# Handing the second halves of a split and part of a weight scaling to GpSimd, with copies a tick later, in a one-core attention layer

## The chip, the cores and the metric

The kernel runs on one core of a Trainium2 chip. The core has a matrix engine (TensorE: PE for its matmuls, PEld for its weight loads), VectorE (DVE), ScalarE (ACT) and GpSimd (POOL). Each works through its own list of instructions in order, and an instruction starts when the semaphores that it names have been set. SyncE (SP) only issues DMA transfers, in order as well; POOL and ACT issue some too. The metric is the time of one execution in device microseconds.

## The reference

One decoder layer on 2048 tokens of width 1024. The input is RMS-normalised and modulated, then projected at once to the inputs of two attention mixers. Mixer A ("FoX") is causal softmax attention of 8 heads of width 64 with a bias from cumulated forget gates. Mixer B is sliding-window attention (128 keys) with 8 query heads, 2 key heads, rotary positions and a sink per head. Both outputs are gated, joined and sent through `w_out`; the result is RMS-normalised, gated and added to the input.

```python
proj = h @ w_in[l]
qa, ka, va, fa, za, qb, kb, vb, zb = jnp.split(proj, split_points, axis=-1)
oa = forgetting_attention(...)          # causal, 8 heads
oa = oa * jax.nn.silu(za)
ob = sliding_window_sink_attention(...) # window 128
ob = ob * jax.nn.silu(zb)
y = jnp.concatenate([oa, ob], axis=-1) @ w_out[l]
x = x + gate[:, None, :] * rms_norm(y, g_post[l])
```

## The kernel before

Every f32 matrix is held as two f16 planes: an upper part (the value rounded to f16) and a lower part (what the rounding left). A product of two such matrices is three f16 matmuls. An upper part is one ACT instruction, a lower part one DVE instruction that subtracts the upper part from the value. The change deals with who makes these parts, and when.

The program is written out by hand, and each engine keeps the order in which the code issues instructions. Work that follows a product is put off with `after(n, f)`: `tick()` counts all such entries down by one and runs those that are due, in the order of their registration.

Three stages matter here.

The *banded stage* is mixer B. Its loop runs over 32 windows (`Pair`: one pair of heads, two blocks of 128 queries). A window has four ticks, with pieces of the projections (`fill`) between them: after the first tick `maxima` (DVE scans L884 and the small L887), after the second `pv` of the window two before (PE L933 into the single PSUM tile `pob`), after the third `exps` (ACT L895) and `split`, which puts off the upper part of the probabilities `sp` (ACT L912) by one tick and the lower part (DVE L917) by two. The window's result goes from `pob` to `on` (DVE L939), is copied to the upper part of `oh` (ACT L948), gets its lower part (DVE L949), and `put` (POOL L945) stores both to `o_d` in DRAM. The projections' weights pass `w_load`, `w_max`, `w_back`, `w_scale`, `w_high` (ACT L273), `w_low` in two halves (DVE L279) and `w_done`; `leads` in `add` says how many pieces (`punits`) ahead of their first use each is issued. POOL also multiplies the rotated halves by the sines (L735), copies the sinks (L882) and issues several DMAs.

The *FoX stage* is mixer A, 8 heads of 20 steps. A step (`Step`) has the scores of two key blocks (PE L1343 and L1344 into the single tile `sta`), the exponential (ACT L1348), for blocks on the diagonal a mask (POOL L1352), the upper part `pha` (ACT L1356), the lower part (DVE L1359), and two steps later `pv` (PE L1369 to L1372 into the single tile `poa`). At the last step of each quarter of the queries (`ci`, of 2, 4, 6 and 8 steps) the result goes to `ona` (DVE L1378), `oha` (ACT L1385, DVE L1386), and by SP (L1382) to `o_d`. A step has two ticks: one behind the exponential, one behind the scores of the next step.

*Head 7*, the last 20 steps, also readies the output product. `w_out` is loaded in 16 pieces (`w_out_load`, SP L1454) and split by `w_out_split`: upper part on ACT (L1459), lower part on DVE (L1460); the table `w_at` says at which step `r` each is split, and the load comes three steps earlier. The first output blocks of 128 rows are readied: `load_o` fetches the planes of `o_d` by transposing DMAs (SP L1475), and `turn` joins them (DVE L1493), multiplies by the gate (DVE L1497), sums squares (ACT L1500), and makes upper and lower parts `oz` (ACT L1511, DVE L1514) for the products (PE L1530).

Last comes the output stage, of which the change touches nothing.

Of the kernel before, what the change touches and what calls it, by code (L numbers as in the profile page):

```python
# [18 lines left out]
P = 128  # L19
# [21 lines left out]
def hybrid_layer(  # L41
# [146 lines left out]
    def after(n, f):  # L188
        late.append([n, f])
# [662 lines left out]
    class Pair:  # L852
# [73 lines left out]
        def pv(self):  # L926
# [10 lines left out]
            def out_():  # L937
                on = onp.tile([P, 2, P], F32, tag="on", name="on")
                V.tensor_tensor(on[:].rearrange("p e (h d) -> p (e h) d", h=2), po[:],  # L939
                                self.rinv[:].unsqueeze(2).broadcast_to([P, 4, 64]), op=ALU.mult)  # L940
                oh = onp.tile([P, 2, 2, P], F16, tag="oh", name="oh")

                def put():
                    rows_ = slice(2 * (i % 4) * P, 2 * (i % 4 + 2) * P)
                    G.dma_start(o_d[i // 4][rows_, (4 + j) * P:(5 + j) * P].rearrange("(m p) c -> p m c", p=P),  # L945
                                oh[:].rearrange("p e a c -> p (e a) c"))

                after(1, lambda: A.activation(oh[:, :, 0], on[:], AF.Copy))  # L948
                after(3, lambda: V.tensor_tensor(oh[:, :, 1], on[:], oh[:, :, 0], op=ALU.subtract))  # L949
                after(4, put)  # L950

            after(1, out_)
# [5 lines left out]
    def add(key, us):  # L958
        if key not in pkeys and key not in ("kb", "vb"):
# [3 lines left out]
                  lambda: w_high(key), lambda: w_low(key, 0), lambda: w_low(key, 1), lambda: w_done(key))  # L963
            if key[:2] == "za":
                leads = leads[:1] + tuple(n - 5 for n in leads[1:])
            if at > N_PRO and (key == "qk0" or key[:2] not in ("qk", "za")):
                leads = (58 if key == "qk0" else 64,) + leads[1:]
            for n, f in enumerate(fs):
# [356 lines left out]
    class Step:  # L1325
# [35 lines left out]
        def pv(self):  # L1361
# [12 lines left out]
            if self.last:  # L1374
                rinv = sm(4, "a_ri")
                V.reciprocal(rinv[:], po[:, :, 64])
                on = op_.tile([P, 4, 64], F32, tag="ona", name="ona")
                V.tensor_tensor(on[:], po[:, :, 0:64], rinv[:].unsqueeze(2).broadcast_to([P, 4, 64]), op=ALU.mult)  # L1378
                oh = op_.tile([P, 4, 2, 64], F16, tag="oha", name="oha")

                def put():
                    SP.dma_start(o_d[self.ci][:, hd * 64:(hd + 1) * 64].rearrange("(m p) d -> p m d", p=P),  # L1382
                                 oh[:].rearrange("p u a d -> p (u a) d"))

                after(1, lambda: A.activation(oh[:, :, 0], on[:], AF.Copy))  # L1385
                after(2, lambda: V.tensor_tensor(oh[:, :, 1], on[:], oh[:, :, 0], op=ALU.subtract))  # L1386
                after(3, put)

        po_ = {}

# [20 lines left out]
    def w_slot(n):  # L1411
        return oio["w"][:, n // KT, n % KT, :]
# [42 lines left out]

    def w_out_split(m):
        k, cc = m % KT, slice((m // KT) * CH, (m // KT + 1) * CH)
        raw, hi = w_raw.pop(m), w_slot(k)[:, cc]
        A.activation(hi, raw, AF.Copy, scale=wsc[:, k:k + 1])  # L1459
        V.scalar_tensor_tensor(w_slot(8 + k)[:, cc], raw, wsc[:, k:k + 1], hi, op0=ALU.mult, op1=ALU.subtract)  # L1460

    class Out:

# [162 lines left out]
    with tc.manual_schedule():  # L1626
# [18 lines left out]
        for _ in range(3):  # L1645
# [2 lines left out]
        p0, p_tot = pos[0], len(punits) - pos[0] - P_LEAD - P_LAST  # L1648
        m_ramp, m_from, m_done = 0, 6 * NS + 7, 7 * NS + 3

        w_at = {2: [0], 3: [1], 4: [2], 5: [3], 6: [4], 8: [5], 10: [6], 11: [7], 12: [8], 13: [9], 14: [10],
                15: [11, 12], 16: [13, 14], 17: [15]}
        w_all = sum(s.w for s in steps[:7 * NS])
        w_acc = 0
        lag[0] = 4
        for s, stp_ in enumerate(steps):
# [43 lines left out]
            tick()  # L1700
            if s >= PV_LAG:
                steps[s - PV_LAG].pv()
            for u in todo[half:]:
                u()
            if r == 3 and hd + 1 < 8:
# [5 lines left out]
                    w_out_load(m)  # L1711
            if hd == 7 and r in (1, 2):
                outs[r - 1].load_z()
            if hd == 7 and r in (5, 6):
                outs[r - 5].load_o()
            if hd == 7 and r in (7, 9):
                outs[(r - 7) // 2].turn(4)
            if s % 4 == 1 and s // 4 <= 32:
# [54 lines left out]
```

## Time and profile before

| | us |
|---|---|
| median of 3 runs | 1162.84 (1162.61 to 1162.91) |
| the profiled execution | 1161.38 |
| its span, first to last instruction | 1159.6 |
| banded stage, about | 205 to 412 |
| FoX stage with its preparation, about | 412 to 923 |
| head 7, about | 923 to 1006 |

The page's second part cuts the span into 40 slices of 29 us. A digit is the busy share of an engine in tenths; PEclk is the granted clock of TensorE, DMA the busy share of the 16 DMA engines.

```profile
PE   5899999989999999999999999999999978999997
DVE  6776568888898858889998899978888878888885
ACT  4666445556665543676767767776776669533331
POOL 2011222233332211111111111102100000000000
PEclk9999999989999999999999999999999999999999
DMA  9646426566788932243323332223212158688853
```

PE is at nine tenths nearly throughout. Dips outside the start stand in the ninth slice (where the clock dips as well) and in the 33rd and 34th, which are head 7. DVE is at eight tenths, POOL nearly idle.

### The profile page before, as it was taken

Reading aid. Unit: us, or ns where it says so; the run is one execution under the profiler, and the core shown is the slowest. Engines: PE = TensorE matmul, PEld = TensorE weight load, DVE = VectorE, ACT = ScalarE, POOL = GpSimd, SP = SyncE. Lnnn points to the kernel's source line nnn. Section 1 sums busy time; section 2 is a strip of 40 time slices with the busy share of each in tenths; the row PEclk is TensorE's granted clock in tenths of the full one; section 3 lists DMA queues with packets and bytes.
Section 4 is the critical chain, followed back from the end, with each engine's and each line's share of the span. In section 5 each row is a group of like instructions: output and inputs, shape, how many; then the busy total and the mean of one; then the engine's idle time right before and its main releaser. Section 6 shows DMA issues by size and latency. Waiting matters only on the chain.

```text
span 1159.6 us, 26925 instructions
## 1 busy us (share of the span) xinstructions
PE 1106.1 (95%) x10386; PEld 638.6 (55%) x10386; DVE 949.7 (82%) x2394; ACT 694.1 (60%) x1188; POOL 174.7 (15%) x317
## 2 busy tenths in 40 slices
PE   5899999989999999999999999999999978999997
PEld 1466657545468956555555555555555545544443
DVE  6776568888898858889998899978888878888885
ACT  4666445556665543676767767776776669533331
POOL 2011222233332211111111111102100000000000
PEclk9999999989999999999999999999999999999999
DMA  9646426566788932243323332223212158688853
GB/s 330 220 138 168 108 69 129 103 149 133 141 153 112 130 85 73 63 113 74 82 68 84 88 74 74 59 53 78 64 39 61 29 135 198 153 202 195 197 172 109
DMA packets 210324, 136.35 MB, mean 118 GB/s; under 512 B 145276, under 2 KB 189348, under 8 KB 210196
## 3 DMA queue, kind: packets, MB, share of 16 engines
q1 hardware_dynamic: 198100, 98.53, 37.8%
q0 software_dynamic: 11616, 35.58, 11.1%
q8 instruction: 81, 1.33, 0.5%
q10 hardware_dynamic: 480, 0.53, 0.2%
q14 instruction: 47, 0.39, 0.1%
HBM read 62.58 MB, written 25.18 MB: 76 GB/s over the span
## 4 chain that ended last, share of the span: by engine, by line
PE 54%; DVE 22%; issue 4%; ACT 4%; DMA 1%; POOL 0%; DVEq 0%; ACTq 0%; POOLq 0%
PE bk L335 18%; PE bk L1530 14%; PE sta L1343 4%; PE sta L1344 4%; PE bk L1294 4%; DVE sp L917 3%; PE poa L1371 2%; PE poa L1372 2%; PE poa L1369 2%; ACT sp L912 2%; DVE a_m L1297 2%; PE bk L353 2%; DVE pha L1359 1%; DVE wmx L230 1%; DVE b_nb L887 1%
## 5 line engine op out<-in xcount | busy, mean ns | idle before, releaser
L1348 ACT ACTIVATE p<-sta,lift,scl_qk 128x1024 f32<-128x1024 f32 (+2 forms) x160 | 171.7, 1073 | 78.8 <-PE sta L1344 74.1
L335 PE MATMUL bk<-hT,wh_qk 128*128 128x512 f16 x768 | 197.9, 378 | 0.0
L1530 PE MATMUL bk<-wohl,oz 128*128 128x512 f16 (+2 forms) x792 | 169.4, 372 | 0.8 <-DVE oz L1514 0.8
L1359 DVE TENSOR_TENSOR pha<-p,pha 128x1024 f16<-128x1024 f32 (+2 forms) x160 | 169.9, 1062 | 0.2 <-ACT pha L1356 0.2
L1356 ACT ACTIVATE pha<-p 128x1024 f16<-128x1024 f32 (+2 forms) x160 | 147.7, 923 | 28.5 <-POOL p L1352 25.8
L1297 DVE TENSOR_REDUCE a_m<-bk 128x1 f32<-128x512 f32 x192 | 130.3, 684 | 32.8 <-PE bk L1294 32.3
L1530 PEld LDWEIGHTS <-oz 128*128 128x128 f16 x792 | 76.0, 99 | 85.5 <-DVE oz L1514 1.3
L1369 PE MATMUL poa<-vt,pha 128*128 128x65 f16 x1088 | 117.7, 194 | 3.0 <-DVE ona L1378 3.0
L1343 PE MATMUL sta<-T 128*128 128x512 f16 (+1 forms) x320 | 110.3, 349 | 9.8 <-ACT p L1348 9.8
L1372 PE MATMUL poa<-vt,pha 128*128 128x65 f16 x1088 | 117.2, 193 | 1.3 <-DVE pha L1359 1.3
L1371 PE MATMUL poa<-vt,pha 128*128 128x64 f16 x1088 | 117.5, 195 | 0.0
L1369 PEld LDWEIGHTS <-pha 128*128 128x128 f16 x1088 | 102.5, 97 | 17.5 <-DVE ona L1378 4.0
L1294 PE MATMUL bk<-T 66*128 66x512 f16 (+2 forms) x320 | 110.5, 348 | 0.2
L1371 PEld LDWEIGHTS <-pha 128*128 128x128 f16 x1088 | 101.7, 98 | 13.5 <-issue 0.3
L1344 PE MATMUL sta<-T 69*128 69x512 f16 (+1 forms) x320 | 108.8, 350 | 0.0
L335 PEld LDWEIGHTS <-wh_qk 128*128 128x128 f16 x768 | 70.2, 97 | 70.0 <-issue 1.3
L1372 PEld LDWEIGHTS <-pha 128*128 128x128 f16 x1088 | 101.5, 99 | 1.6 <-DVE pha L1359 1.6
L335 PE MATMUL bk<-hT,wh_za 128*128 128x512 f16 x384 | 101.1, 381 | 0.0
L1352 POOL TENSOR_SCALAR_AFFINE_SELECT p<-p 128x256 f32<-128x256 f32 x64 | 31.6, 494 | 424.8 <-ACT p L1348 412.3
L335 PE MATMUL bk<-hT,wh_qb 128*128 128x512 f16 x384 | 91.1, 385 | 4.4 <-DVE wh_qb L279 4.4
L353 PE MATMUL bk<-wh_va,hT 128*128 128x128 f16 x1536 | 93.1, 219 | 2.0 <-DVE wh_va L279 2.0
L353 PEld LDWEIGHTS <-hT 128*128 128x128 f16 x1536 | 87.6, 98 | 7.3 <-issue 4.9
(501 smaller groups left out, 1905.5 us busy)
## 6 DMA issues: line engine op xcount, KB each, us to landing
hT<-in_x_dram SPq DMA_DIRECT2D x20, 512.0 KB
wa<-in_w_ada_dram SPq DMA_DIRECT2D x16, 512.0 KB
T<-stq SPq DMA_DIRECT2D x128, 64.0 KB
T<-z_d SPq DMA_DIRECT2D x16, 512.0 KB
z_d<-tz POOLq DMA_DIRECT2D x30, 256.0 KB, 3.0
out_dram<-hT POOLq DMA_DIRECT2D x15, 512.0 KB, 5.2
xt<-in_x_dram SPq DMA_DIRECT2D x12, 512.0 KB
qs<-qf SPq DMA_DIRECT2D x80, 64.0 KB
```

The lines of the kernel that those rows point to most:

```text
L335: PE.matmul(ps, whl[:, a, k, :], hT[ci][:, b, k, :], start=(k == 0 and n == 0), stop=(k == KT - 1 and n == 2))
L353: PE.matmul(ps[:, u * P:(u + 1) * P], hT[ci][:, a, k, u * P:(u + 1) * P], whl[:, b, k, :], start=(k == 0 and n == 0), stop=(k == KT - 1 an ...
L1294: PE.matmul(mx[:, :w], T[0:XM, 0, i * P:(i + 1) * P], T[0:XM, 2, pc * CH:pc * CH + w], start=True, stop=True)
L1297: V.tensor_reduce(m3[:, u, pc:pc + 1], mx[:, :w], axis=AX.X, op=ALU.max)
L1343: PE.matmul(self.st[:, o:o + w], T[:, 3, kb_], T[:, 1, qc], start=True, stop=False)
L1344: PE.matmul(self.st[:, o:o + w], T[0:XR, 2, kb_], T[0:XR, 0, qc], start=False, stop=True)
L1348: A.activation(self.p32[:, :self.w], self.st[:, :self.w], AF.Exp, scale=scl[f"qk{self.hd}"][:], bias=lift[:])
L1359: V.tensor_tensor(self.ph[:, 1, :self.w], self.p32[:, :self.w], self.ph[:, 0, :self.w], op=ALU.subtract)
L1369: PE.matmul(po[:, u, :], ph[:, 0, pq], vt[:, b, hd, 0:65], start=(self.first and n == 0 and u == 0), stop=False)
L1371: PE.matmul(po[:, u, 0:64], ph[:, 0, pq], vt[:, b, hd, 65:VW], start=False, stop=False)
L1372: PE.matmul(po[:, u, :], ph[:, 1, pq], vt[:, b, hd, 0:65], start=False, stop=(self.last and n == len(self.blocks) - 1))
L1530: PE.matmul(py, self.hl[:, i, k, :], w_slot(8 * j + k)[:, cc], start=(k == 0 and m_ == 0), stop=(k == KT - 1 and m_ == 2))
```

## The change

Five edits.

1. Banded stage: the lower part of `oh` is made by POOL in `put`, directly ahead of the store that POOL issues. The ACT copy ahead of it comes one tick later.
2. The halves of `w_low` for the projections `qb1` to `qb3` are issued at 8 and 6 pieces ahead of their use, in place of 6 and 4; `w_done` at 5 in place of 3.
3. FoX stage: the lower part of `oha` is made by POOL; copy, lower part and store are each one tick later; and `oha` has two buffers, for even and odd quarters.
4. Head 7: eleven of the sixteen upper parts of `w_out` (all but pieces 0, 2, 3, 6 and 7) are made by POOL. The lower parts stay with DVE, but move from ahead of a step's first pieces to behind its `pv` (`w_out_low`). Pieces 11 and 13 come one step earlier.
5. The planes for the first two output blocks are fetched behind steps 6 and 7, in place of 5 and 6.

```diff
@@ Pair.pv, out_ @@
                 def put():
+                    G.tensor_tensor(oh[:, :, 1], on[:], oh[:, :, 0], op=ALU.subtract)
                     rows_ = slice(2 * (i % 4) * P, 2 * (i % 4 + 2) * P)
                     G.dma_start(o_d[i // 4][rows_, (4 + j) * P:(5 + j) * P].rearrange("(m p) c -> p m c", p=P),
                                 oh[:].rearrange("p e a c -> p (e a) c"))
 
-                after(1, lambda: A.activation(oh[:, :, 0], on[:], AF.Copy))
-                after(3, lambda: V.tensor_tensor(oh[:, :, 1], on[:], oh[:, :, 0], op=ALU.subtract))
+                after(2, lambda: A.activation(oh[:, :, 0], on[:], AF.Copy))
                 after(4, put)
@@ add @@
+            if key[:2] == "qb" and at > N_PRO:
+                leads = leads[:5] + (8, 6, 5)
@@ Step.pv @@
-                oh = op_.tile([P, 4, 2, 64], F16, tag="oha", name="oha")
+                oh = op_.tile([P, 4, 2, 64], F16, tag=f"oha{self.ci % 2}", name="oha")
...
-                after(1, lambda: A.activation(oh[:, :, 0], on[:], AF.Copy))
-                after(2, lambda: V.tensor_tensor(oh[:, :, 1], on[:], oh[:, :, 0], op=ALU.subtract))
-                after(3, put)
+                after(2, lambda: A.activation(oh[:, :, 0], on[:], AF.Copy))
+                after(3, lambda: G.tensor_tensor(oh[:, :, 1], on[:], oh[:, :, 0], op=ALU.subtract))
+                after(4, put)
@@ w_out_split @@
-        raw, hi = w_raw.pop(m), w_slot(k)[:, cc]
-        A.activation(hi, raw, AF.Copy, scale=wsc[:, k:k + 1])
-        V.scalar_tensor_tensor(w_slot(8 + k)[:, cc], raw, wsc[:, k:k + 1], hi, op0=ALU.mult, op1=ALU.subtract)
+        raw, hi = w_raw[m], w_slot(k)[:, cc]
+        if m in (0, 2, 3, 6, 7):
+            A.activation(hi, raw, AF.Copy, scale=wsc[:, k:k + 1])
+        else:
+            G.tensor_scalar(hi, raw, wsc[:, k:k + 1], None, op0=ALU.mult)
+
+    def w_out_low(m):
+        k, cc = m % KT, slice((m // KT) * CH, (m // KT + 1) * CH)
+        V.scalar_tensor_tensor(w_slot(8 + k)[:, cc], w_raw.pop(m), wsc[:, k:k + 1], w_slot(k)[:, cc],
+                               op0=ALU.mult, op1=ALU.subtract)
@@ the loop over steps @@
-        w_at = {2: [0], 3: [1], 4: [2], 5: [3], 6: [4], 8: [5], 10: [6], 11: [7], 12: [8], 13: [9], 14: [10],
-                15: [11, 12], 16: [13, 14], 17: [15]}
+        w_at = {2: [0], 3: [1], 4: [2], 5: [3], 6: [4], 8: [5], 10: [6], 11: [7], 12: [8], 13: [9], 14: [10, 11],
+                15: [12, 13], 16: [14], 17: [15]}
...
             if s >= PV_LAG:
                 steps[s - PV_LAG].pv()
+            if hd == 7:
+                for m in w_at.get(r, []):
+                    w_out_low(m)
...
-            if hd == 7 and r in (5, 6):
-                outs[r - 5].load_o()
+            if hd == 7 and r in (6, 7):
+                outs[r - 6].load_o()
```

The order of PE's own instructions is the same in both programs. Three places elsewhere show what moves.

First place: ACT in the banded stage, at the window whose probabilities `sm__3076` are split. Before, ACT stands so (L895 the exponentials, L273 the upper part of the weights, L912 the upper part of the probabilities):

```order
L895 ACTIVATE sm__3076,b_rs<-sm__3076,b_nb 128x257 x2
L273 ACTIVATE wh_qb_3153<-wr_qb_2330,w_sw 128x1024
L948 ACTIVATE oh<-on 128x2x128
L912 ACTIVATE sp_1978<-sm__3076 128x256
L912 ACTIVATE sp_1978<-sm__3076 128x512
L723 ACTIVATE qf<-bk_139 128x512
```

And now:

```order
L895 ACTIVATE sm__3076,b_rs<-sm__3076,b_nb 128x257 x2
L273 ACTIVATE wh_qb_3153<-wr_qb_2330,w_sw 128x1024
L912 ACTIVATE sp_1978<-sm__3076 128x256
L912 ACTIVATE sp_1978<-sm__3076 128x512
L723 ACTIVATE qf<-bk_139 128x512
L949 ACTIVATE oh<-on 128x2x128
```

The copy `oh<-on` no longer stands between the exponentials and the upper part `sp`; it follows both, ahead of the next window's exponentials.

Second place: DVE, at the same window and the next, whose maxima are scanned by L884 (some rows of equal kind between are left out at the start and the end). Before:

```order
L939 TENSOR_TENSOR on<-pob,b_ri 128x256
L917 TENSOR_TENSOR sp_1979<-sm__3076,sp_1978 128x256
L917 TENSOR_TENSOR sp_1979<-sm__3076,sp_1978 128x512
L921 RECIPROCAL b_ri<-b_rs 128x4
L742 SCALAR_TENSOR_TENSOR qc<-bk_139,cosT 128x512
```

Behind these come the four scans of the next window, and then:

```order
L887 TENSOR_SCALAR b_nb<-b_m 128x2
L279 SCALAR_TENSOR_TENSOR wh_qb_3153<-wr_qb_2330,w_sw,wh_qb_3153 128x512
L736 TENSOR_TENSOR qc<-qc,qs 128x512
L949 TENSOR_TENSOR oh<-on,oh 128x2x128
L279 SCALAR_TENSOR_TENSOR wh_qb_3153<-wr_qb_2330,w_sw,wh_qb_3153 128x512
```

Now the stretch ahead of the scans reads:

```order
L939 TENSOR_TENSOR on<-pob,b_ri 128x256
L279 SCALAR_TENSOR_TENSOR wh_qb_3153<-wr_qb_2330,w_sw,wh_qb_3153 128x512
L917 TENSOR_TENSOR sp_1979<-sm__3076,sp_1978 128x256
L917 TENSOR_TENSOR sp_1979<-sm__3076,sp_1978 128x512
L921 RECIPROCAL b_ri<-b_rs 128x4
```

The first half of `wh_qb` has moved from behind the scans to ahead of L917; the second half stands directly behind the scans, and `oh<-on,oh` has left DVE.

Third place: ACT in head 7, from the upper part of step 2 to the upper part of step 4 (L1348 and L1350 are the exponentials before and now, L1459 and L1462 the parts of `w_out`). Before:

```order
L1459 ACTIVATE wohl<-wo_14210,wsc 128x512
L1356 ACTIVATE pha<-p_14256 128x1024
L1348 ACTIVATE p_14314<-sta,lift,scl_qk_13021 128x1024
L1459 ACTIVATE wohl<-wo_14212,wsc 128x512
L1356 ACTIVATE pha<-p_14314 128x1024
L1348 ACTIVATE p_14349<-sta,lift,scl_qk_13021 128x896
L1385 ACTIVATE oha<-ona 128x4x64
L385 ACTIVATE gz<-bk_139,cz_za_13337 128x512
L1256 ACTIVATE rw<-bk_6465 8x128
L1459 ACTIVATE wohl<-wo_14214,wsc 128x512
L1356 ACTIVATE pha<-p_14349 128x896
```

And now:

```order
L1462 ACTIVATE wohl<-wo_14210,wsc 128x512
L1358 ACTIVATE pha<-p_14256 128x1024
L1387 ACTIVATE oha<-ona 128x4x64
L1350 ACTIVATE p_14313<-sta,lift,scl_qk_13021 128x1024
L1358 ACTIVATE pha<-p_14313 128x1024
L1350 ACTIVATE p_14349<-sta,lift,scl_qk_13021 128x896
L385 ACTIVATE gz<-bk_139,cz_za_13336 128x512
L1258 ACTIVATE rw<-bk_6465 8x128
L1462 ACTIVATE wohl<-wo_14214,wsc 128x512
L1358 ACTIVATE pha<-p_14349 128x896
L1387 ACTIVATE oha<-ona 128x4x64
```

One part of `w_out` has left this stretch of ACT, the copy of head 6's last quarter now stands here (it was just ahead of the stretch), and the copy of head 7's first quarter has moved behind step 4's upper part.

## The prediction

> **What bounds the kernel now.** I cut the span by stage and look at PE's busy time first: the program's PE instructions and their order do not change, so the kernel can only become faster where PE stands idle or runs at a lower clock.
>
> ```profile
> core 0: us, PE busy (x) PEld busy (x) DVE busy (x) ACT busy (x) POOL busy (x), PEclk, DMA share, GB/s
> 231.00:235.00 4.00, 0.20 (x1) 0.00 (x0) 3.93 (x15) 1.62 (x7) 0.30 (x2) 0.78 0.52 100
> 235.00:241.00 6.00, 5.91 (x25) 2.29 (x26) 4.53 (x11) 3.03 (x7) 1.22 (x2) 0.58 0.46 102
> 205.00:412.00 207.00, 195.46 (x2440) 131.17 (x2438) 176.18 (x525) 125.45 (x320) 60.40 (x117) 0.98 0.74 133
> 412.00:923.00 511.00, 506.25 (x4967) 285.05 (x4966) 440.31 (x1009) 345.59 (x478) 65.32 (x115) 1.00 0.29 69
> 923.00:1006.00 83.00, 72.62 (x754) 42.12 (x752) 68.49 (x122) 62.60 (x88) 7.14 (x13) 0.96 0.63 153
> ```
>
> PE idles 207.00 - 195.46 = 11.5 us in the banded stage, 511.00 - 506.25 = 4.8 in the FoX stage and 83.00 - 72.62 = 10.4 in head 7. To this comes the clock: behind the longest stall of the banded stage 6 us were granted 0.58, a loss of 6 x 0.42 = 2.5; head 7 at 0.96 loses about 83 x 0.04 = 3.3. All together 32.5 us, the most that the change could bring. PE's waits say who was late:
>
> ```profile
> PE sta L1343 <- ACT p L1348: 9.8, 9, 2.9
> ...
> PE bk L335 <- DVE wh_qb L279: 4.4, 2, 3.9
> PE poa L1369 <- DVE ona L1378: 3.0, 4, 1.2
> PE pob L933 <- DVE on L939: 2.5, 4, 1.2
> PE bk L353 <- DVE wh_va L279: 2.0, 3, 0.9
> ...
> PE bk L1243 <- DVE vt L362: 1.4, 1, 1.4
> ...
> PE poa L1372 <- DVE pha L1359: 1.3, 2, 1.0
> ...
> PE pob L933 <- DMA ptb<-sp: 1.2, 2, 0.7
> ...
> PE bk L1530 <- DVE oz L1514: 0.8, 1, 0.8
> ```
>
> In the banded stage 4.4 + 2.5 + 2.0 + 1.4 = 10.3 us of the 11.5 fall to DVE and 1.2 to a DMA. DVE is busy for 176.18 of 207 us there, so why is it late? Its own waits and ACT's answer:
>
> ```profile
> DVE sp L917 <- ACT sp L912: 26.7, 22, 1.4
> ...
> ACT oh L948 <- DVE on L939: 23.9, 26, 2.2
> ```
>
> The two form a loop. ACT makes the copy `oh` ahead of `sp` and waits for DVE's `on`; DVE, right behind `on`, then waits for `sp`, up to 1.4 us: the copy (0.42) and `sp` itself (1.04). One window shows it, with the late weights behind:
>
> ```profile
> 228.59 0.42 ACT L948 ACTIVATE oh<-on 128x256 f16<-128x256 f32 x1 [1.00 <-DVE on L939]
> 228.91 0.92 ACT L912 ACTIVATE sp<-sm__3076 128x256 f16<-128x256 f32 x2
> ...
> 229.32 1.26 POOL L735 TENSOR_TENSOR qs<-qs,sinT 128x512 f32<-128x512 f32 x1 [0.70 <-DMA qs<-qf]
> ...
> 229.34 2.12 DVE L917 TENSOR_TENSOR sp<-sm__3076,sp 128x256 f16<-128x256 f32 x2 [0.79 <-ACT sp L912]
> ...
> 234.29 0.74 DVE L279 SCALAR_TENSOR_TENSOR wh_qb<-wr_qb,w_sw,wh_qb 128x512 f16<-128x512 f32 x1
> ```
>
> **Durations.** The operations that leave an engine, and the two POOL operations nearest to the new ones:
>
> ```profile
> L949 DVE TENSOR_TENSOR oh<-on,oh 128x256 f16<-128x256 f32 x32 | 13.4, 418 | 0.0
> L1386 DVE TENSOR_TENSOR oha<-ona,oha 128x256 f16<-128x256 f32 x32 | 13.3, 415 | 0.0
> L1459 ACT ACTIVATE wohl<-hT,wsc 128x512 f16<-128x512 f32 x11 | 7.6, 711 | 0.0
> ...
> L735 POOL TENSOR_TENSOR qs<-qs,sinT x20: 1259/1263/2018, 57.4 to 356.7; 128x512 f32<-128x512 f32 x20
> ...
> L1352 POOL TENSOR_SCALAR_AFFINE_SELECT p<-p x64: 396/402/1247, 450.0 to 999.8; 128x256 f32<-128x256 f32 x64
> ```
>
> POOL's subtraction of 128x256 is not in the trace. It lies between the mask of the same size (0.40, one input) and the product of twice the size (1.26); I take half of the latter, 0.65. POOL's scaling of 128x512 lies between twice the mask (0.80) and 1.26; it has one input, so I take 0.9.
>
> The Trainium skill (GPSIMD Engine Reference, Engine selection) advises against this move: elementwise work with two inputs is about twice as slow on GpSimd as on VectorE. By that page the subtraction is an estimated 2 x 0.42 = 0.84 us; the sum below would be the same, since POOL is idle for 147 of 207 us.
>
> **Edits 1 and 2, banded stage.** Removed from DVE: 32 x 0.418 = 13.4 us, a few of them just ahead of this stretch. On ACT the copy moves behind `sp`: DVE's wait for `sp` should lose most of its 26.7 us, for when DVE comes from `on`, ACT has only had the exponentials ahead of `sp`. I count 15. The first half of `wh_qb` now stands ahead of L917, where DVE waited 0.79 us anyway, instead of at 234.29 behind four scans; PE stood from about 231 to 235 for it. The second half comes right behind the scans, about when PE, running, reaches its fifth piece.
>
> What is added: 32 subtractions on POOL (21 us) and the wait of each store for one. Behind a store POOL has the sink copies, the sine products and small DMAs. The subtraction takes the place of a wait, since POOL stood idle for DVE's `oh` before each store, and the copy that it needs is made earlier in the window than DVE's part was. So its queue should not be later. But POOL and DVE hinder each other. At 229.32 L735 began, at 229.34 L917 on DVE, and the pair took 2.12 us. Undisturbed it takes half:
>
> ```profile
> L917 DVE TENSOR_TENSOR sp<-sm__3941,sp 128x256 f16<-128x256 f32 (+1 forms) x2 | 1.0, 550 | 0.0
> ```
>
> That cost 1.1 us for an overlap with 1.26. A subtraction of 0.65 that begins first can thus cost DVE nothing to 0.65; I take 0.25, or 8 us in all.
>
> DVE nets 13 + 15 - 8 = 20 us, spread over the windows; the longest lateness is 3.9. So its 10.3 us of stalls go, with the 2.5 of slow clock, except for about 1.0 of L362, which at the end of the stage hangs on PE's own last products. The DMA's 1.2 loses half, for `sp` is ready earlier. I leave 1 for new collisions: 10.3 + 2.5 + 0.6 - 1.0 - 1.0 = **11.4 gained**, bounds 5 and 14. If DVE stays late, all of it is lost; the cover is POOL's idle time.
>
> **Edit 3, FoX stage.** DVE loses 0.415 for each quarter, 27 of the 32 here (five of them are finished in head 7): 11.2 us. As many POOL subtractions may hold it, 27 x 0.25 = 7. Of the 4.8 idle, 1.8 is `ona` (DVE) and most of the rest is ACT's exponential, which now no longer stands behind a copy that waits for `ona`. I take **1.0 gained**, bounds -3 and 3.
>
> **Edits 3 to 5, head 7.** Here the rows are followed in time:
>
> ```profile
> 938.44 0.72 ACT L1459 ACTIVATE wohl<-wo,wsc 128x512 f16<-128x512 f32 x1 [1.92 <-DMA wo<-in_w_out_dram]
> ...
> 940.02 1.19 ACT L1348 ACTIVATE p<-sta,lift,scl_qk 128x1024 f32<-128x1024 f32 x1
> ...
> 942.67 1.09 ACT L1348 ACTIVATE p<-sta,lift,scl_qk 128x896 f32<-128x896 f32 x1
> 946.76 0.42 ACT L1385 ACTIVATE oha<-ona 128x256 f16<-128x256 f32 x1 [3.00 <-DMA o_d<-oha]
> 947.08 0.67 ACT L385 ACTIVATE gz<-bk,cz_za 128x512 f32<-128x512 f32 x1
> ...
> 948.42 0.93 ACT L1356 ACTIVATE pha<-p 128x896 f16<-128x896 f32 x1
> 949.26 0.65 ACT L1348 ACTIVATE p<-sta,lift,scl_qk 128x384 f32<-128x384 f32 x1
> ...
> 949.66 0.39 SPq L1382 DMA_DIRECT2D o_d<-oha  x1
> 952.31 5.96 SPq L1475 DMA_TRANSPOSE T<-o_d  x4
> ...
> 958.05 1.22 DVE L1493 TENSOR_TENSOR osum<-T 128x1024 f32<-128x1024 f16 x1
> ...
> 960.55 1.06 ACT L1500 ACTIVATE hT<-T 128x1024 bf16<-128x1024 f32 x1 [0.27 <-DVE T L1497]
> ...
> 961.61 1.19 ACT L1348 ACTIVATE p<-sta,lift,scl_qk 128x1024 f32<-128x1024 f32 x1
> ```
>
> The first stall, ACT's 1.92 for the load of piece 0, stays: piece 0 is still ACT's. A copy of 0.42 now stands behind that step's upper part, but piece 1 (0.71) is gone from ACT, so step 4's exponential stands where it did and ends near 943.7. The 3.00 us that ACT waits for the old store of `oha` go with the second buffer. From the start of `gz` to the end of step 4's upper part took 947.08 to 949.35, or 2.27; now that is 943.7 to 946.0. The copy then ends near 946.4 and step 5's exponential (0.65) near 947.1, in place of 949.9.
>
> But the output block's planes hang on this copy. It began at 946.76 and begins now at 946.0. Ahead of the subtraction POOL has the mask of step 5 (to 947.5); the subtraction ends at 948.2 and the store is issued near 948.4, in place of 949.66. Store to transposes took 949.66 to 952.31, transposes to `osum` 5.7: so `osum` can begin at about 956.8, 1.2 earlier, and through gate (L1497) and squares (L1500) step 9's exponential at 960.4 in place of 961.61. That is the exponential for which PE stalls last. That the fetch is issued a step later costs nothing by itself, as SP waits only for the store. So I gain 1.2 up to here, and DVE now waits for the planes.
>
> Past this point the eleven parts (11 x 0.71 = 7.8 us) leave ACT mostly where PE hardly waits for it; `oz` (0.8) comes earlier, as `w_out_low` moved behind it, and about 1 us of slow clock goes. POOL's scalings (11 x 0.9) can hold DVE. Sum **3.0 gained**, bounds -1 and 9.
>
> **Sum.** 11.4 + 1.0 + 3.0 = 15.4 from the profiled execution's own 1161.38 us is 1146.0. The median of the runs shown is 1162.84, 1.46 above it, so I add that: 1147.4, put at **1147.5**.
>
> **Rivals.** *The planes' fetch gives head 7 nothing* (say 20%): POOL's subtraction is held by DVE's `pha`, the store is no earlier than before, or lands later. For it speaks the chain above, in which every link got slower but the wait; against it the 3.00 us that are surely gone. Time: 1162.84 - 11.4 - 1.0 = 1150.4, or up to 2 more.
>
> *The DMAs set the banded stage's pace* (8%): they are busy 0.74 of it, and `ptb` was late twice. Then a stall by DVE becomes one by `ptb`, and with 1 to 3 us from elsewhere the time is 1160 to 1162, no change. Against it: its waits are 1.2 us now.
>
> *POOL holds DVE, and the kernel is slower* (8%). The place is head 7 and the diagonal steps, where nearly all that DVE does has two SBUF inputs. DVE is busy 68.5 of 83 us; if each of eleven scalings and five subtractions stops it for its whole length, at the upper bounds 11 x 1.26 + 5 x 1.26 = 20 us less 2 saved, DVE needs 86.6, more than the stage has: +3.6. FoX would lose another 28 x (0.65 - 0.42) = 6 at most, of DVE time that is partly idle. If the banded stage gains nothing by the same mechanism, the result is 1166 to 1170. It decides where a POOL operation costs DVE more than 0.42 plus what the freed wait for `sp` gives, some 0.5 a window. L735's longest times (2018 against a median of 1263) say that POOL is the one held in other cases, which speaks against it. The Trainium skill (SBUF — State Buffer, Who interferes with whom) has the rule behind this rival: a VectorE instruction with two SBUF inputs and a GpSimd instruction that reads SBUF exclude each other, and the later one waits for the whole of the first. The pair at 229.32 agrees; how often they meet, the rule doesn't say.
>
> **How the numbers follow.** Forecast 64%, the first rival 20, the other two 8 each. The range reaches from 1140, where the banded stage and head 7 give 14 and 8, to 1159, where the banded stage gives 5 and the rest nothing or a little less. A measurement of this kernel can tell about 0.2%, or 2.3 us, from no change: forecast and first rival are faster, the second rival is the same, the third slower.
>
> **What would show it.** Right: PE's waits for `wh_qb` and `on` gone, the clock at 1.00 from 235 on, DVE's wait for ACT's `sp` well under 10 us, ACT's wait for `o_d<-oha` gone, and DVE or ACT waiting for the planes near step 8. Wrong: many L917 or L1359 above their usual length beside POOL rows, `ptb` high in PE's waits, or a gain in head 7 beyond 6 us, which would mean that the chain of the planes doesn't bind.

## The result, and the profile after

The changed kernel takes 1149.43 us (median of 4 runs, 1148.6 to 1150.55), the kernel before in the same comparison 1162.72. The ratio is 0.9891, with a 95% interval of 0.9874 to 0.9908. The profiled execution took 1150.14 us, its span is 1148.4. The sum of the terms said 1146.0 for it, so 11.2 us were gained of the 15.4 counted.

The windows of the changed kernel, cut at the same places of the program as before (everything behind the banded stage stands about 13 us earlier), and a piece of head 7 that is read below:

```profile
core 0: us, PE busy (x) PEld busy (x) DVE busy (x) ACT busy (x) POOL busy (x), PEclk, DMA share, GB/s
205.00:399.00 194.00, 191.31 (x2439) 130.51 (x2438) 165.91 (x491) 124.27 (x318) 78.75 (x141) 1.00 0.70 141
399.00:910.00 511.00, 505.62 (x4966) 284.77 (x4964) 434.44 (x979) 348.23 (x478) 92.55 (x142) 1.00 0.29 69
910.00:995.00 85.00, 74.17 (x755) 42.76 (x754) 72.32 (x119) 57.39 (x77) 34.27 (x28) 0.94 0.62 150
949.00:954.00 5.00, 4.24 (x33) 2.73 (x33) 3.63 (x6) 4.31 (x5) 0.75 (x1) 0.50 0.86 240
```

In the banded stage PE idles 194.00 - 191.31 = 2.7 us in place of 11.5, at a clock of 1.00. FoX is as it was. Head 7 still idles 85.00 - 74.17 = 10.8 us, hardly more than the 10.4 before, and 5 us of it were granted a clock of 0.50. At 0.94 the stage loses about 85 x 0.06 = 5.1 us to the clock, where it lost 3.3 before. PE's waits in the changed kernel (sum, times, longest) name what is left:

```profile
PE sta L1345 <- ACT p L1350: 11.3, 9, 5.1
...
PE pob L933 <- DVE on L939: 1.6, 1, 1.6
PE bk L1539 <- DVE wohl L1468: 1.4, 1, 1.4
...
PE bk L1245 <- DVE vt L362: 1.1, 1, 1.1
```

The waits for `wh_qb`, `wh_va` and `ptb` are gone, `on` is late once instead of four times. New are one wait of 5.1 us for an exponential and one of 1.4 for a lower part of `w_out`. DVE's and ACT's own waits in the changed kernel:

```profile
DVE sp L917 <- ACT sp L912: 13.7, 14, 2.9
...
DVE osum L1502 <- DMA T<-o_d: 3.0, 1, 3.0
```

```profile
ACT wohl L1462 <- DMA wo<-in_w_out_dram: 3.2, 1, 3.2
...
ACT oh L949 <- DVE on L939: 2.1, 3, 0.8
```

The loop of the two engines is loosened: ACT waits 2.1 us for `on` instead of 23.9, DVE 13.7 for `sp` instead of 26.7. ACT's wait for the old store of `oha` is gone, and DVE now waits 3.0 us for the planes.

**Where the 11.2 us come from.** PE runs the same 10386 matmuls in the same order in every kernel here, so the n-th of one trace can be set against the n-th of another. I take the matmuls that begin in the trace of before at 205, 431 and 920 us, and the last one. How much earlier the changed kernel is at these four, each less the one ahead of it, is what a stage gained:

```
us gained against the trace of before    start   banded    FoX    head 7 to end
predicted                                   -     11.4     1.0     3.0
changed kernel                             0.4    12.3     0.2    -1.8
```

The first two stages came out within 1 us of what was said; head 7 lost where it should have won. Its rows in the changed kernel (the start in us, the duration, in brackets the idle time ahead):

```profile
930.21 1.10 ACT L1350 ACTIVATE p<-sta,lift,scl_qk 128x896 f32<-128x896 f32 x1 [0.65 <-PE sta L1346]
...
934.18 0.40 ACT L1387 ACTIVATE oha<-ona 128x256 f16<-128x256 f32 x1
...
935.78 0.75 DVE L1468 SCALAR_TENSOR_TENSOR wohl<-wo,wsc,wohl 128x512 f16<-128x512 f32 x1
...
935.92 1.15 POOL L1388 TENSOR_TENSOR oha<-ona,oha 128x256 f16<-128x256 f32 x1
...
937.09 0.39 SPq L1384 DMA_DIRECT2D o_d<-oha  x1
940.13 2.64 SPq L1484 DMA_TRANSPOSE T<-o_d  x2
...
944.95 1.22 DVE L1502 TENSOR_TENSOR osum<-T 128x1024 f32<-128x1024 f16 x1 [2.99 <-DMA T<-o_d]
...
947.47 1.06 ACT L1509 ACTIVATE hT<-T 128x1024 bf16<-128x1024 f32 x1 [3.83 <-DVE T L1506]
...
948.52 1.19 ACT L1350 ACTIVATE p<-sta,lift,scl_qk 128x1024 f32<-128x1024 f32 x1
949.76 0.59 PE L1345 MATMUL sta<-T 128*128 128x512 f16 x1 [5.05 <-ACT p L1350]
```

This is the chain of the prediction. Up to 943 us ACT has caught up; then it stands idle for 3.83 us, because the squares L1509 wait for the planes and step 9's exponential stands behind them in ACT's queue. All that ACT saved earlier in head 7 is spent in this one wait, and behind PE's stall of 5.05 comes the slow clock. Matched PE instructions show the same: inside head 7 the changed kernel is 3.3 us ahead just before this stall and 0.2 ahead behind it. The 1.8 us are lost later, 1.0 at 977.46 and 1.6 at 985.10, with 0.8 coming back. At 977.46 it is again the squares: two of the moved lower parts (L1468, 1.84 us from 971.59) stand on DVE between `osum` and the gate (L1506, at 973.35), ACT is idle for 2.47 us until the gate is through, and the exponential follows behind the squares.

### The profile page after: what moved, and what is told of

Its sections match the earlier page's. It is cut to its first block, busy times and chain, and to the rows that moved or that the text cites. A ratio compares the mean times of both kernels' runs of the same rounds, so it can differ in the third digit from the quotient of the medians.

```text
span 1148.4 us, 26956 instructions
## 1 busy us (share of the span) xinstructions
PE 1104.2 (96%) x10386; PEld 638.5 (56%) x10386; DVE 939.5 (82%) x2330; ACT 692.8 (60%) x1177; POOL 252.4 (22%) x392
## 4 chain that ended last, share of the span: by engine, by line
PE 82%; DVE 8%; DMA 4%; ACT 3%; issue 2%; SPq 0%; POOL 0%; DVEq 0%; ACTq 0%
PE bk L335 33%; PE bk L1539 13%; PE bk L353 7%; PE sta L1345 5%; PE bk L1296 4%; PE sta L1346 4%; PE poa L1373 3%; PE poa L1374 2%; PE poa L1371 2%; PE pss L870 2%; PE pob L933 2%; DMA wa<-in_w_ada_dram 2%; PE bk L776 1%; DVE pha L1361 1%; DVE a_m L1299 1%
## 5 line engine op out<-in xcount | busy, mean ns | idle before, releaser
L1350 ACT ACTIVATE p<-sta,lift,scl_qk 128x1024 f32<-128x1024 f32 (+2 forms) x160 | 171.7, 1073 | 85.4 <-PE sta L1346 81.4
L1361 DVE TENSOR_TENSOR pha<-p,pha 128x1024 f16<-128x1024 f32 (+2 forms) x160 | 173.0, 1081 | 0.0
L1345 PE MATMUL sta<-T 128*128 128x512 f16 (+1 forms) x320 | 110.7, 351 | 11.4 <-ACT p L1350 11.3
L335 PE MATMUL bk<-hT,wh_zb 128*128 128x512 f16 x384 | 90.8, 379 | 0.0
```

What stands on the lines that cost most here:

```text
L335: PE.matmul(ps, whl[:, a, k, :], hT[ci][:, b, k, :], start=(k == 0 and n == 0), stop=(k == KT - 1 and n == 2))
L1345: PE.matmul(self.st[:, o:o + w], T[:, 3, kb_], T[:, 1, qc], start=True, stop=False)
L1350: A.activation(self.p32[:, :self.w], self.st[:, :self.w], AF.Exp, scale=scl[f"qk{self.hd}"][:], bias=lift[:])
L1361: V.tensor_tensor(self.ph[:, 1, :self.w], self.p32[:, :self.w], self.ph[:, 0, :self.w], op=ALU.subtract)
```

## The experiments

Twelve kernels, all compared with the kernel before over several runs. First their gains by stage, measured as above on one execution each (what each kernel is stands below):

```
us gained against the trace of before    start   banded    FoX    head 7    ratio of times, 95% interval
changed kernel                             0.4    12.3     0.2    -1.8      0.9891, 0.9874 to 0.9908
e1_banded_only                             0.5    11.6     0.0    -0.5      0.9904, 0.9889 to 0.9918
e2_fox_out_only                            0.5    -1.2     0.2    -1.9      1.0005, 0.9996 to 1.0014
e3_scale_on_act                            0.3    11.9     0.2    -1.1      0.9896, 0.9881 to 0.9911
e4_planes_early                            0.6    13.0    -1.6     1.2      0.9883, 0.9867 to 0.9899
e5_copy_later                              0.2    14.3     0.0    -0.3      0.9871, 0.9855 to 0.9888
e6_pool_sub                                0.4     6.3     0.0    -2.2      0.9951, 0.9936 to 0.9966
e7_leads                                  -1.1     1.9     0.0    -0.2      1.0013, 1.0001 to 1.0024
e9_squares_later                           0.6    12.7    -1.6     2.5      0.9863, 0.9848 to 0.9878
e10_low15_first                            0.4    12.2     0.2     0.3      0.9877, 0.9861 to 0.9894
e12_copy_later_head7                       0.5    14.5    -1.6     3.5      0.9838, 0.9822 to 0.9854
e13_no_pool                                0.0    14.5     0.0    -1.1      0.9856, 0.9839 to 0.9872
e14_fox_sub_dve                            0.6    14.4     0.0     3.7      0.9835, 0.9822 to 0.9848
```

How far a stage's figure can be trusted shows where its code is that of before: the banded stage of e2 lost 1.2, and head 7 of e1, e5, e6 and e7 lost 0.2 to 2.2. So the trace of before was at the good end for head 7, and a difference of up to 2 us in one execution of either stage means little alone. FoX, where its code is that of before, repeats within 0.1.

**e1 and e2: which half of the change makes the gain.** e1 has edits 1 and 2 alone, e2 edits 3 to 5 alone.

> Edits 1 and 2 alone on the kernel before: the banded stage's subtraction on POOL, its copy a tick later, w_qb's halves earlier. Theory: these two edits make the whole gain, and edits 3 to 5 cost 1 to 2 us in head 7. Matched PE instructions stand 0.4 us earlier at 205 us and 12.7 earlier at 431, so the time is about 1162.8 - 12.3 = 1150.5 (1149.5 to 1151.5), PE's waits for wh_qb and on are gone, and head 7 has before's stalls again. Rival: edits 3 to 5 also gain, and the kernel without them is 1152 or more.

> Edits 3 to 5 alone: the changed kernel with the banded stage as before. Theory: head 7 ends about 1.8 us later than before and FoX is equal within 0.3, so 1164.4 (1163 to 1166); ACT's waits for the old store of oha are gone and a PE stall of about 5 us stands ahead of step 10's scores. Rival: the loss in head 7 comes only from how the loads meet once the banded stage is 12 us shorter; then these edits alone are at 1162.8 or below.

e1 took 1151.19 us, e2 1163.16 (before in this group: 1162.51). The banded edits make the whole gain; edits 3 to 5 alone change nothing that can be measured, so the times don't decide between e2's theory and its rival. ACT's waits for the store of `oha` are gone in e2, and PE stands 5.2 us ahead of step 10's scores, with the banded stage as before, so this stall does not come from an earlier arrival.

**e3: POOL's slow scalings.** All sixteen upper parts of `w_out` on ACT again:

```diff
-        if m in (0, 2, 3, 6, 7):
-            A.activation(hi, raw, AF.Copy, scale=wsc[:, k:k + 1])
-        else:
-            G.tensor_scalar(hi, raw, wsc[:, k:k + 1], None, op0=ALU.mult)
+        A.activation(hi, raw, AF.Copy, scale=wsc[:, k:k + 1])
```

> The changed kernel with all sixteen upper parts of w_out on ACT again, the lower parts and the new list of steps kept. Theory: POOL's scalings take 1.6 to 2.9 us, more than twice what I took, and make w_out_low late behind step 12: two PE stalls of 1.0 and 1.6 go, the stall of 5.2 ahead of step 10 stays, since ACT is idle 3.8 us there: 1149.4 - 2.5 = 1147 (1146 to 1148.5). Rival: eleven more parts on ACT (7.8 us) make the exponentials late and the time is 1150 or more.

It took 1150.38 us, neither better nor worse than the changed kernel. That is the rival's number, but its reason isn't in the trace: PE's waits for the exponential sum to 11.1 us, against 11.3 in the changed kernel. The stall at 977.46 falls from 0.8 to 0.3 us. The theory was wrong on the other one: the wait for a lower part of `w_out`, which I had put down to POOL, is still there in PE's waits of e3:

```profile
PE bk L1536 <- DVE wohl L1465: 1.4, 1, 1.4
```

**e10: where that lower part is made.** In the changed kernel DVE's rows ahead of the stall at 985.1 are these:

```profile
983.01 1.22 DVE L1502 TENSOR_TENSOR osum<-T 128x1024 f32<-128x1024 f16 x1
984.15 0.89 DVE L1468 SCALAR_TENSOR_TENSOR wohl<-hT,wsc,wohl 128x512 f16<-128x512 f32 x1
```

Piece 15 is made behind the next block's `osum`; in the kernel before it was made ahead of it. e10 puts this one piece back:

```diff
                 for m in w_at.get(r, []):
                     w_out_split(m)
+                    if r == 17:
+                        w_out_low(m)
...
-            if hd == 7:
+            if hd == 7 and r != 17:
                 for m in w_at.get(r, []):
                     w_out_low(m)
```

> The changed kernel, with w_out's last lower part (piece 15, step 17) made where the kernel before made it, in the step's first half ahead of osum. Theory: with the upper parts on ACT the stall of 1.59 us on this lower part stayed, so it is the new place and not POOL's speed that makes it late; here it goes, with at most 0.8 of it coming back at the last products: 1148.2 (1147.5 to 1149). Rival: DVE then waits for POOL's last scaling, and the stall stays: 1149.4 or more.

It took 1147.97 us, the stall is gone, and head 7 is 2.1 us better than in the changed kernel (the ratios of the two overlap). So the place made it late, not POOL's speed. Not all of the 2.1 comes from it: matched PE instructions put 1.3 ahead of this place, where the changed kernel's clock is 0.81 from 926 to 935 us and e10's 1.00, and behind it a wait for `pha` takes 0.8 back.

**e4 and e9: the planes.** e4 makes copy, subtraction and store of `oha` a tick earlier and fetches the planes at steps 5 and 6 again; e9 adds one line:

```diff
-                after(2, lambda: A.activation(oh[:, :, 0], on[:], AF.Copy))
-                after(3, lambda: G.tensor_tensor(oh[:, :, 1], on[:], oh[:, :, 0], op=ALU.subtract))
-                after(4, put)
+                after(1, lambda: A.activation(oh[:, :, 0], on[:], AF.Copy))
+                after(2, lambda: G.tensor_tensor(oh[:, :, 1], on[:], oh[:, :, 0], op=ALU.subtract))
+                after(3, put)
...
-            if hd == 7 and r in (6, 7):
-                outs[r - 6].load_o()
+            if hd == 7 and r in (5, 6):
+                outs[r - 5].load_o()
...  (the rest in e9 alone)
-            after(3 if lag > 4 else 2, squares_)
+            after(3, squares_)
```

> The changed kernel with copy, subtraction and store of oha one tick earlier (1, 2, 3, as before, still POOL and two buffers), and the planes fetched at steps 5 and 6 again. Theory: the planes' chain (copy, POOL's subtraction behind the mask, store, transposes, osum, squares) sets step 9's exponential; a tick is about 2 us, so the stall of 5.2 shrinks by 2 to 4 us: 1146.5 (1145.5 to 1148). Rival: the chain is bound by the transposes and the loads between them, the stall stays at 4 to 5 us and the time at 1149 to 1150.

> The kernel of e4 (oha a tick earlier, planes at steps 5 and 6), with the squares of each output block one tick later for the blocks that are turned within four ticks: on ACT step 9's exponential then stands ahead of the squares that wait for the planes. PE's order is the same. Theory: PE's stall of 3.9 us ahead of step 10's scores is only ACT's queue order; the exponential no longer waits for the planes, and PE is next held where it needs the squares' sum, 0.5 to 1.5 us: 1146 (1145 to 1147.3). Rival: the planes themselves are late for the products, and the stall moves to oz or to the squares' sum in full: 1148.5.

e4 took 1148.63 us, between the two ranges. Its stall is 3.7 us instead of 5.1: the store is issued at 934.04 in place of 937.09, but `osum` begins at 943.49 in place of 944.95, so of 3 us only 1.5 arrived with the planes. Theory and rival each hold half. e9 took 1147.64 us, between its theory and its rival (before in its group: 1164.04; its ratio and e4's overlap, so the reading is of the trace). PE no longer stalls ahead of step 10's scores; it is held next by these two:

```profile
PE bk L1539 <- DVE oz L1523: 2.7, 1, 2.7
...
PE bk L1513 <- ACT hT L1509: 2.1, 1, 2.1
```

So the exponential was late only because of its place in ACT's queue, behind squares that waited for a DMA. The planes themselves are late too: 2.1 us of it comes back at the squares' sum, more than the 0.5 to 1.5 expected, and `oz` at 2.7 is new. Head 7 gains 2.5 all the same, and its window says why:

```profile
920.00:1000.00 80.00, 69.65 (x686) 38.50 (x685) 71.12 (x123) 53.72 (x72) 34.48 (x27) 1.00 0.69 173
```

PE idles 80.00 - 69.65 = 10.4 us, nearly as much as in the changed kernel, but at a clock of 1.00: in this trace the shorter stalls save the slow clock and hardly any idle time.

**e5, e6, e7: the banded edits one by one.** Each on the kernel before:

```diff
e5  -                after(1, lambda: A.activation(oh[:, :, 0], on[:], AF.Copy))
    +                after(2, lambda: A.activation(oh[:, :, 0], on[:], AF.Copy))

e6  +                    G.tensor_tensor(oh[:, :, 1], on[:], oh[:, :, 0], op=ALU.subtract)
    -                after(3, lambda: V.tensor_tensor(oh[:, :, 1], on[:], oh[:, :, 0], op=ALU.subtract))

e7  +            if key[:2] == "qb" and at > N_PRO:
    +                leads = leads[:5] + (8, 6, 5)
```

> The kernel before, with only the banded stage's copy a tick later (behind sp on ACT); DVE keeps the subtraction at its tick, w_qb's halves stay. Theory: the wait of DVE for ACT's sp is as large a relief as the subtraction, and the two hold PE up through DVE's lateness alike; DVE's wait for sp falls from 26.7 to below 15 us and the time from 1162.5 by 4 to 8 us: 1156.5. Rival: the copy's place gives nothing by itself, because DVE then waits for the copy at its own subtraction, a tick later: 1161.5 or more.

> The kernel before, with only the banded stage's subtraction moved to POOL; the copy stays ahead of sp, w_qb's halves stay. Theory: 13 us go from DVE, up to 8 come back where POOL holds it, so a third of the gain: 1159 (1156 to 1161). Rival: POOL holds DVE as long as the subtraction took there: 1162 or more.

> The kernel before, with only w_qb's halves 2 and 1 units earlier. Theory: DVE stays as late as it was, so of the 3.9 us of the longest stall and the 2.5 of slow clock behind it a part goes here and comes back at the next piece that DVE owes: 1160 (1158 to 1162). Rival: this edit alone makes most of the gain, since the longest stall and the slow clock were 6 to 7 of the 12: below 1157.

The medians are 1147.19, 1156.69 and 1164.05 us (before in this group: 1162.79). One number, the copy's tick, gains 15.6 us, and its stage gains 14.3: more than all banded edits together. This I did not expect; both the theory (4 to 8) and the rival (1 or less) missed it. In e5 DVE's and ACT's waits and the window of the stage read:

```profile
DVE sp L917 <- ACT sp L912: 8.2, 11, 1.2
```

```profile
ACT oh L948 <- DVE on L939: 3.5, 4, 1.1
```

```profile
205.00:397.60 192.60, 191.19 (x2439) 130.45 (x2438) 171.07 (x521) 123.64 (x318) 59.29 (x113) 1.00 0.71 142
```

DVE works 171.07 us here against 165.91 in the changed kernel, and PE idles only 192.60 - 191.19 = 1.4 us, all of it the wait for `vt` at the stage's end. So opening the loop is enough to remove every stall that DVE caused; that DVE's load counts too, as long as the loop is there, e6 shows. e6 leaves the copy in the loop and takes the subtraction off DVE. DVE waits for `sp` as long as before:

```profile
DVE sp L917 <- ACT sp L912: 27.2, 22, 1.6
```

It gains 6.1 us, where DVE was late: more than the theory's third, inside its range. e7 missed its theory of 1158 to 1162 and shows in PE's waits that an order cannot mend lateness:

```profile
PE pob L933 <- DVE on L939: 4.8, 6, 1.0
...
PE pob L933 <- DMA ptb<-sp: 2.6, 3, 1.1
```

The wait for `wh_qb` fell from 4.4 to 0.5 us, and `on` went from 2.5 to 4.8, `ptb` from 1.2 to 2.6. Its trace shows 1.9 us gained in the stage, but that execution, 1160.58, was the lowest of twelve; the times show nothing, and I go by the times.

**What POOL's subtraction and edit 2 cost in the banded stage.** The banded stage gains 11.6 to 13.0 us in the six kernels that have the later copy with POOL's subtraction and edit 2 (changed kernel, e1, e3, e4, e9, e10), and 14.3 to 14.5 in the four that have the later copy without them (e5, e12, e13, e14). Matched with e5, the changed kernel loses its ground at one place, PE's wait for `on` at 282.8. Its rows there:

```profile
279.41 1.16 DVE L887 TENSOR_SCALAR b_nb<-b_m 128x2 f32<-128x2 f32 x1
...
281.74 0.69 DVE L736 TENSOR_TENSOR qc<-qc,qs 128x512 f32<-128x512 f32 x1
282.35 0.42 DVE L939 TENSOR_TENSOR on<-pob,b_ri 128x256 f32<-128x256 f32 x1
...
279.61 0.31 POOL L882 COPY sm__3941<-snk 128x2 f32<-128x2 f32 x2
279.87 0.67 POOL L944 TENSOR_TENSOR oh<-on,oh 128x256 f16<-128x256 f32 x1
```

L887 takes 0.17 us when alone; here it ends only when POOL's copies and its subtraction are through, 1 us later, and `on` and PE follow (1.6 us of stall). No run has the later copy and POOL's subtraction without edit 2, so the 2 us belong to the two together; that the subtraction is the larger part is read from these rows alone.

**e12, e13, e14: put together.** e12 takes e5's later copy (subtraction on DVE, `w_qb` as before), e9's head 7 and e10's piece 15. e13 has three lines on the kernel before and no new work on POOL: the banded copy's tick, two buffers for `oha`, the squares' tick. e14 is e12 with one word more:

```diff
-                after(2, lambda: G.tensor_tensor(oh[:, :, 1], on[:], oh[:, :, 0], op=ALU.subtract))
+                after(2, lambda: (G if hd == 7 else V).tensor_tensor(oh[:, :, 1], on[:], oh[:, :, 0], op=ALU.subtract))
```

> The later copy of e5 in the banded stage (subtraction on DVE, w_qb as before), with e9's head 7 and piece 15's lower part in the first half as in e10. Theory: the gains are of different stages and add up: e5's banded stage ends 14.4 us earlier; head 7 gives 2 to 4 more: 1144.5 (1143 to 1146). Rival: head 7 holds a fixed end (loads, planes) and an earlier start gives nothing: 1147 or more.

> Three small edits on the kernel before and nothing on POOL: the banded copy a tick later, two buffers for oha, the squares a tick later. Theory: the 3.3 us that ACT waited for the old store of oha go, and PE's stall ahead of step 10's scores (2.1) with them; some of it comes back where oz is late (2.5 in e5): 1145 (1143.5 to 1146.5). Rival: without POOL's help ACT and DVE are too full in head 7, and it is no faster than e5: 1147.

> The kernel of e12, with DVE making oha's lower part in heads 0 to 6 and POOL only in head 7. Theory: where the subtraction stands a tick earlier (e4, e9, e12), matched PE instructions lose 1.5 us between 430 and 780 us, because POOL's subtraction meets DVE's pha and holds it; with DVE's own subtraction (e5, e13) they lose nothing. Here the 1.5 us come back and head 7 keeps its gain: 1143 (1142 to 1144.5). Rival: the loss in FoX comes from the copy's tick on ACT and stays: 1144.6.

e12 took 1144.61 us and e13 1147.10 (before in their group: 1164.04), e14 1143.22 (before: 1162.49). The gains of the stages add up. e13 is no faster than e5, as its rival said: the stall ahead of step 10's scores is down to 0.5 us there too, but PE's wait for `oz`, 2.4 us in e5, is 3.7. Whether ACT and DVE being full is the reason, as the rival has it, was not shown. What e12's head 7 has over it (the subtractions and scalings on POOL, the order of the lower parts) was not taken apart. e14's ratio of 0.9835 (0.9822 to 0.9848) lies below the changed kernel's interval; e12 and e14 can't be told apart by their times, but the traces show FoX's 1.6 us come back. One place of it, worth 0.5, in e12:

```profile
523.11 1.52 POOL L1386 TENSOR_TENSOR oha<-ona,oha 128x256 f16<-128x256 f32 x1 [2.42 <-ACT oha L1385]
524.58 0.60 POOL L247 DMA_DIRECT2D mxr<-mx_d  x1
525.19 0.79 POOL L1352 TENSOR_SCALAR_AFFINE_SELECT p<-p 128x256 f32<-128x256 f32 x1
...
526.02 0.52 ACT L1356 ACTIVATE pha<-p 128x384 f16<-128x384 f32 x1 [1.43 <-POOL p L1352]
```

And in e14:

```profile
524.46 0.85 POOL L1352 TENSOR_SCALAR_AFFINE_SELECT p<-p 128x256 f32<-128x256 f32 x1 [3.21 <-ACT p L1348]
...
525.35 0.52 ACT L1356 ACTIVATE pha<-p 128x384 f16<-128x384 f32 x1 [0.96 <-POOL p L1352]
```

The subtraction, stretched to 1.52 us beside DVE, and the DMA issue behind it stand on POOL ahead of the mask of the diagonal step (e14 issued that DMA at 520.68, before the mask was due); ACT's `pha` and the exponential behind it follow later. I had written that POOL holds DVE's `pha`; what PE feels here is POOL's own queue.

## Why the prediction came out as it did

**What bounds the kernel** was read rightly: PE's waits and the slow clock behind the longest one. Nearly all of the gain came from the stage and the waits named.

**Edits 1 and 2, 11.4 counted, 12.3 measured.** The sum was right: it is the size of PE's stalls, and any relief of DVE that is large enough removes them. How the relief is made up was wrong. I added 13 us of subtractions gone and 15 of waits, less 8 for POOL. The waits for `sp` fell by 26.7 - 13.7 = 13.0, near the 15. But e5 shows that ending the waits is enough: with the subtraction kept DVE does 5 us more work and is late nowhere. The subtractions' leaving, worth 6 us by itself in e6, bought nothing behind that, and POOL's subtraction with edit 2 cost about 2 us. Likewise edit 2 was counted as needed for `wh_qb`; that stall is gone in e5 without it. The failed step is "DVE nets 13 + 15 - 8 = 20 us": terms with the same stall to remove don't add. The gains of e5 and e6 in the stage sum to 20.6 us where there were 14 to get (11.5 idle, 2.5 of slow clock).

**POOL's subtraction, 0.65 taken.** The groups of POOL's operations in the changed kernel (shortest, median and longest ns):

```profile
L944 POOL TENSOR_TENSOR oh<-on,oh x32: 657/668/1640, 182.3 to 397.6; 128x256 f16<-128x256 f32 x32
L1388 POOL TENSOR_TENSOR oha<-ona,oha x32: 658/670/1706, 459.3 to 997.7; 128x256 f16<-128x256 f32 x32
L1464 POOL TENSOR_SCALAR wohl<-hT,wsc x9: 1626/2133/2909, 939.5 to 977.5; 128x512 f16<-128x512 f32 x9
```

The subtraction has a median of 0.67 us. The estimate from the Trainium skill (GPSIMD Engine Reference, Engine selection), 0.84, was too high: 0.67 against DVE's 0.42 is 1.6 times, not twice. **The scaling**, taken at 0.9 with a bound of 1.26, takes 1.63 to 2.91 in these nine and 1.56 and 1.86 in the two on `wo`, far outside. Giving it back to ACT made the kernel no faster (e3). How much of it is the operation itself, one scaling bounds. It began at 937.05 and took 1.86. DVE's `pha` beside it was through at 937.48, and DVE then waited for the scaling, which ended at 938.91: 1.43 us of it ran with DVE idle. The shortest took 1.56 in all. Its own length lies between these two, above the bound; what goes beyond 1.56 came beside DVE.

**FoX, 1.0 counted, 0.2 measured**, within its bounds of -3 to 3.

**Head 7, 3.0 counted, -1.8 measured**, below the bound of -1, and here the prediction failed. By the times of e2, edits 3 to 5 together are 0.6 us slower than nothing (1.6 slower to 0.5 faster), where 1.0 + 3.0 was counted. Set back to the clock of before (12.9 us earlier), the chain was to run: step 4's exponential ends 943.7, copy ends 946.4, subtraction ends 948.2, store 948.4, `osum` 956.8, step 9's exponential 960.4. It ran: 944.2, 947.5, 950.0, 950.0, 957.9, 961.4. Against before (`osum` 958.05, exponential 961.61) that is 0.2 gained, not 1.2. Step 4's exponential waited 0.65 for PE and came 0.5 late; up to the copy another 0.6 was lost, as `gz` ahead of it waited for PE too; and the subtraction, 1.15 instead of 0.65 beside DVE, lost 0.7 with the mask ahead of it. The second failed step is "the eleven parts leave ACT mostly where PE hardly waits" with `w_out_low` counted only for the good of `oz`: its new place made piece 15 late by 1.6 us, and the squares ahead of 977.46 by 1.0. The 1 us of slow clock that was to go did not go: the stage's loss to the clock rose from 3.3 to 5.1 us. That the chain of the planes binds, which the text said, is what happened; I then priced the links too short. The first rival (head 7 gives nothing) named this mechanism; set against the profiled execution it is 1161.38 - 12.4 = 1149.0 or up to 2 more, and 1150.14 was measured, so it is the better account. Part of the miss is the trace of before: head 7 with unchanged code was up to 2.2 us worse in other executions.

**The other rivals.** The DMAs did not set the pace: `ptb` is not in PE's waits of the changed kernel. POOL holding DVE was real but small: at most the 2 us in the banded stage. Four of L917's 28 large rows took 1.63 to 1.84 us instead of 1.22. FoX's 1.6, where the subtraction stood a tick earlier, were at the place read POOL's own queue.

**The signs.** Of the five signs of being right four came: `wh_qb` gone from PE's waits with `on` down to one, the clock at 1.00 in the banded stage, ACT's wait for the old store gone, DVE (2.99) and ACT (3.83) waiting for the planes. The fifth did not: DVE waits 13.7 us for `sp`, not well under 10. In e5, where DVE keeps its subtraction, it is 8.2.

**The sum.** The profiled execution is 4.1 us above 1146.0. The 1.46 us that I added for the median did not apply: here the median, 1149.43, lies 0.7 below the profiled run. So the median missed by 1.9 us only because these 2.2 us went the other way, which is luck.

## What to carry to other kernels

When two engines wait for each other in turn, look for the one instruction that closes the loop and move that alone, before moving load from one engine to another: here one tick of one copy gave as much as all five edits. Gains that remove the same stall don't add, so try each edit alone. And an instruction that must wait for a DMA belongs behind those that other engines wait for, in its engine's queue.

## What the runs showed of the hardware

- A 128x512 scaling by a column of factors takes POOL 1.43 to 1.56 us by itself (worked out above), ACT 0.71 for a piece of the same size (L1462: 704 to 721 ns). The 128x512 product of two tiles on POOL (L735) took 1.26, so the count of inputs is a poor guide there.
- A tiny instruction of DVE can be held much longer than a large one: L887, 128x2, normally 0.17 us, took up to 1.31 beside POOL, while L917, 1.22 alone, went to 1.75 and 1.84.
- Whether POOL and DVE take turns in the order they come is not settled here. At 194.47 POOL's subtraction began 0.03 us ahead of L917, which then took 1.75; at 201.60 it began 0.07 us behind L917, and L917 was again the one stretched (1.84), POOL taking 0.68 both times. The first agrees with the rule of the Trainium skill (SBUF — State Buffer, Who interferes with whom) that the later one waits. The second does not, if these two rows are all that counts; but when L917 began, POOL was still issuing a DMA (L236, to 201.58).

```profile
194.50 1.75 DVE L917 TENSOR_TENSOR sp<-sm__2509,sp 128x1024 f16<-128x1024 f32 x1
...
201.53 1.84 DVE L917 TENSOR_TENSOR sp<-sm__2621,sp 128x1024 f16<-128x1024 f32 x1
...
194.47 0.68 POOL L944 TENSOR_TENSOR oh<-on,oh 128x256 f16<-128x256 f32 x1
...
201.00 0.58 POOL L236 DMA_DIRECT2D mx_d<-wmt  x1 [4.39 <-DVE wmt L232]
201.60 0.68 POOL L944 TENSOR_TENSOR oh<-on,oh 128x256 f16<-128x256 f32 x1
```
